# A transformer stack in fp32: the program opens with the MLA input projection, and the memory keys and values come after it

## The chip, the core and the metric

The kernel runs on 1 core of one Trainium2 chip. The metric is the device time of one execution in microseconds (us), as the median of a few runs. Before the change it is 1916.09 us (3 runs, 1915.34 to 1917.74).

Engines are named as in the profile: PE is TensorE's matmuls, PEld its weight loads, DVE VectorE, ACT ScalarE, POOL GpSimd, SP the engine that issues the DMAs.

## What is computed

Two blocks on x (512 tokens, 1024 wide), in fp32. The first block has two layers, each with a mixer, a cross-attention to 256 memory tokens, an output projection and an MLP. The mixer of layer 0 is MLA, that of layer 1 sliding-window attention. The second block (sparse attention, convolutions, FFN) is not touched. What matters here, cut from the reference:

```python
mem_n = rmsnorm(mem, mem_norm_g)
hn = rmsnorm(x, attn_norm_g[0])
proj = hn @ mla_w_in                  # 1024 x 928: c_q 384, c_kv 256, k_r 32, q_cross 256
q  = rmsnorm(c_q, q_norm_g) @ w_uq
kv = rmsnorm(c_kv, kv_norm_g) @ w_ukv
k_r = rope(k_r, positions)
kv_mem = mem_n @ w_mem_kv[i]          # for both layers i, 1024 x 512
cross = softmax(q_cross @ k_mem.T) @ v_mem
```

## The kernel before

Every product of two fp32 matrices is three matmuls: both operands are split into a high part `h` and a low part `l`, and `mm` issues h·h, h·l and l·h into one PSUM bank. Activations stand with features on partitions: 8 tiles of 128 x 512 for x (256 for memory). A projection (`dense`) gives a bank to 128 output columns and runs over 8 contraction tiles, so 24 matmuls make one block.

Weights lie in HBM in the order in which they are used (`_weight_plan`), in chunks of 128 x 512 (256 KB). For each chunk SP loads `raw` (4 buffers), ACT casts `h`, and DVE subtracts `l = raw - h` (8 buffers of each). For the keys in `POOL_KEYS` POOL does the subtraction. `Norm.tile` splits a scaled tile (ACT `h`, DVE `l`) and squares it on ACT, and adds the square to a sum. `finish` gives the sum to PE for column sums (`pst<-ones`), to DVE for a chain of 15 small instructions that make the reciprocal root (`rsqrt`), to DVE for a diagonal matrix and to PE for a broadcast (`pst<-pgf,ones`). ACT copies that to the tile R, and each projection's result is multiplied by R when it leaves its bank.

The order on each engine is set by a list scheduler in the kernel (`Trace.schedule`): among instructions that are ready by its own costs, the one recorded first goes first. `later(n)` shifts a place in the record by n. Each engine then runs its list strictly in that order.

In `build`, `setup` loads the constants, memory and x; `mem_phase` norms memory and makes keys (`memk`) and values (`memv`) of both layers; `first_block` norms x with `Norm.all` (name `n0`), then `mla` runs the five blocks `mla_c0` to `mla_c4` (three at first in parallel, then one by one), the norms `nq` and `nkv`, then `mla_kr`, `mla_x0`, `mla_x1` (the cross queries), then cross-attention and MLA.

In the trace nearly all instructions have one line, that of the recorder; names tell them apart. Pages of SBUF are `pgf` and `pgr`, the PSUM banks `psd` (3), `pss` (2), `pst` (2) and `pso` (1), weight parts `raw`, `h` and `l`.

Of the kernel before, what the change touches and what calls it, by code (L numbers as in the profile page):

```python
# [19 lines left out]
KD = 8  # L20
# [7 lines left out]
X_AT = 200  # L28
POOL_KEYS = ("swa_q", "n_a", "uq", "ukv", "mla_")
MEM_AT = 0  # L30
# [8 lines left out]
def _weight_plan():  # L39
    plan = []  # L40

    def add(key, k, c, fn):
        plan.append((key, k, c, fn))
# [16 lines left out]
    add("mla_kr", KD, 64, kr)  # L60
# [66 lines left out]
def _weight_layout():  # L127
    plan = _weight_plan()
    blocks, chunks, off, cur = {}, [], 0, 0
    keyk = {}  # L130
    for key, k, c, _ in plan:
        keyk[key] = k
        for j in range(k):
            if cur + c > CHUNK:
                chunks.append((off, cur))
                off += P * cur
                cur = 0
            blocks[key, j] = (len(chunks), cur, c)
            cur += c
    chunks.append((off, cur))  # L140
    off += P * cur
    return plan, blocks, chunks, off, keyk


def pack_weights(a):
    plan, blocks, chunks, total, _ = _weight_layout()
    w = np.empty(total, np.float32)
    views = [w[o:o + P * n].reshape(P, n) for o, n in chunks]
    for key, k, c, fn in plan:
        m = fn(a)  # L150
        for j in range(k):
            ch, co, _ = blocks[key, j]
            views[ch][:, co:co + c] = m[j * P:(j + 1) * P]
    return w
# [381 lines left out]
class Norm:  # L536
    def __init__(self, net, src, gains, d, name):
# [6 lines left out]
    def tile(self, m, split=True):  # L544
        net, nc = self.net, self.net.nc
        if split:
            self.h[m], self.l[m] = net.split_scaled(self.src[m], self.gains[m], f"{self.name}s{m}")
# [64 lines left out]
class Net:  # L612
    def __init__(self, ctx, tc, aps):
# [11 lines left out]
        for key, k, _, _ in self.plan:  # L625
            for j in range(k):
                self.first_key.setdefault(self.blocks[key, j][0], key)
# [21 lines left out]
    def load_chunk(self, i):  # L649
        nc = self.nc  # L650
# [24 lines left out]
    def split_scaled(self, src, g, name):  # L675
        nc = self.nc
        n = src.shape[-1]
        h = self.pg(name + "h", FR)[:, :n]
        l = self.pg(name + "l", FR)[:, :n]
# [55 lines left out]
    def dense(self, jobs, xh, xl, il=1, n=S, ks=None):  # L735
        i = 0
        while i < len(jobs):
            grp = jobs[i:i + (il if i == 0 else 1)]
            i += len(grp)
            pss = [self.ps("d") for _ in grp]  # L740
# [24 lines left out]
    def setup(self):  # L765
# [6 lines left out]
        mem = [self.pg(f"mem{j}") for j in range(4)]  # L772
        nc.sync.dma_start(self.vecs, self.a["vec"])
        for j in range(4):
            with nc.later(MEM_AT * j):
                nc.sync.dma_start(mem[j], self.a["memT"][:, 2 * j:2 * j + 2, :].rearrange("p a b -> p (a b)"))
        with nc.later(CST_AT):
            nc.sync.dma_start(self.cst, self.a["cst"])
        self.X = [self.keep(f"x{m}", [P, S]) for m in range(KD)]
        for m in range(KD):  # L780
            with nc.later(X_AT):
                nc.sync.dma_start(self.X[m], self.a["xT"][:, m, :])
# [6 lines left out]
        self.memsrc = [mem[k // 2][:, (k % 2) * 256:(k % 2) * 256 + 256] for k in range(KD)]  # L789
# [40 lines left out]
    def mem_phase(self):  # L830
        nc = self.nc
        nm = Norm(self, self.memsrc, self.gains("mem_norm_g", 0, KD), 1024, "mem")
        nm.all()
        self.memk, self.memv = [], []
        for i in range(2):
# [9 lines left out]
            self.dense([(f"memk{i}_{m}", P, kev(m)) for m in range(2)], nm.h, nm.l, il=2 if i == 0 else 1, n=NMEM)  # L845
# [113 lines left out]
    def mla(self, nx, osh, osl):  # L959
# [9 lines left out]
        self.dense([(f"mla_c{m}", P, cev(m)) for m in range(5)], nx.h, nx.l, il=3)  # L969
        nq = Norm(self, c[:3], self.gains("mla_q_norm_g", 0, 3), 384, "nq")  # L970
        nkv = Norm(self, c[3:], self.gains("mla_kv_norm_g", 0, 2), 256, "nkv")
        ch, cl = [], []
        for nn, cc, g in ((nq, c[:3], nq.gains), (nkv, c[3:], nkv.gains)):
# [706 lines left out]
```

## Time and profile before

| | |
|---|---|
| median of 3 runs | 1916.09 us |
| span of the profiled execution | 1914.9 us |
| PE busy | 1856.5 us (97%), 8749 matmuls |
| DVE busy | 1169.7 us (61%) |
| ACT busy | 835.5 us (44%) |
| POOL busy | 388.9 us (20%) |
| mean granted TensorE clock | 0.991 |

The span runs from the first to the last instruction; the page gives no other time for that execution, so what lies around the span is told by the median alone, which is 1.2 us above it. PE is busy nearly everywhere, so time is to be looked for where PE waits or runs at its lower clock.

### The profile page before, as it was taken

What the parts mean: (1) busy time and instruction counts of PE and PEld (TensorE: products, weight loads), DVE (VectorE), ACT (ScalarE), POOL (GpSimd) and SP (SyncE); (2) the same over time, 40 slices, a digit from 0 to 9 for tenths busy, and PEclk for the clock granted to TensorE, in tenths of its full rate; (3) what the DMA queues carried; (4) which work ended last, traced back from release to release, by engine and by line L of the source; (5) the groups of instructions that cost most, each with busy time, mean ns of one, the idle gap of its engine ahead of it and who ended that gap; (6) DMA issues with size and microseconds to landing.
All of it is one profiled execution on the core that took longest, in us unless ns stands there. A gap on an engine that the chain in (4) does not pass through costs nothing.

```text
span 1914.9 us, 25100 instructions
## 1 busy us (share of the span) xinstructions
PE 1856.5 (97%) x8749; PEld 1527.4 (80%) x8749; DVE 1169.7 (61%) x2268; ACT 835.5 (44%) x1674; POOL 388.9 (20%) x431
## 2 busy tenths in 40 slices
PE   6789999999999998999999999999999999999999
PEld 6567688888888876888888887778888888888887
DVE  8588875444446688654444356777755567774652
ACT  7378644332424677443323243447633333332321
POOL 4454320000001354100000040455300122110100
PEclk9899999999999999999999999899999999999999
DMA  6211133333333210333333322311133233333332
GB/s 214 79 49 50 45 94 104 95 99 95 98 99 95 78 56 17 99 105 95 98 98 95 99 81 58 105 45 45 56 94 99 89 93 105 94 99 99 94 99 76
DMA packets 92150, 166.98 MB, mean 87 GB/s; under 512 B 10612, under 2 KB 12408, under 8 KB 92024
## 3 DMA queue, kind: packets, MB, share of 16 engines
q1 hardware_dynamic: 92024, 165.40, 28.8%
q8 instruction: 68, 1.11, 0.2%
q14 instruction: 58, 0.48, 0.1%
HBM read 161.68 MB, written 2.10 MB: 86 GB/s over the span
## 4 chain that ended last, share of the span: by engine, by line
PE 86%; DVE 7%; ACT 3%; issue 2%; POOL 1%; DMA 1%; SPq 0%; DVEq 0%; POOLq 0%; ACTq 0%
PE psd L415 77%; PE pst L415 3%; DVE pgf L415 3%; PE pso L415 3%; PE pss L415 3%; DVE pgr L415 2%; DVE sm L415 1%; ACT pgf L415 1%; ACT pgr L415 1%; POOL pgf L415 1%; DVE l L415 1%; ACT h L415 1%; DMA raw<-w 0%; DVE x L415 0%; DMA pgf<-memT 0%
## 5 line engine op out<-in xcount | busy, mean ns | idle before, releaser
L415 PE MATMUL psd<-pgr,h 128*128 128x512 f32 (+2 forms) x4622 | 1448.8, 393 | 16.2 <-ACT h L415 11.6
L415 PEld LDWEIGHTS psd<-pgr,h 128*128 128x128 f32 (+1 forms) x4622 | 867.4, 189 | 196.0 <-ACT h L415 11.6
L415 PE MATMUL psd<-pgr,l 128*128 128x512 f32 (+2 forms) x2311 | 905.8, 392 | 0.8 <-DVE l L415 0.8
L415 DVE TENSOR_TENSOR l<-raw,h 128x512 fp32r<-128x512 f32 (+1 forms) x536 | 419.4, 785 | 453.9 <-ACT h L415 451.9
L415 ACT CAST h<-raw 128x512 fp32r<-128x512 f32 (+2 forms) x601 | 368.6, 616 | 700.8 <-PE psd L415 618.5
L415 PEld LDWEIGHTS psd<-pgr,l 128*128 128x128 f32 (+1 forms) x2311 | 436.5, 189 | 91.2 <-issue 3.5
L415 POOL TENSOR_TENSOR pgf<-pgf,pgf 128x512 f32<-128x512 f32 (+1 forms) x106 | 142.3, 1345 | 1078.8 <-ACT pgf L415 770.9
L415 DVE TENSOR_TENSOR pgr<-pgf,pgr 128x512 fp32r<-128x512 f32 (+4 forms) x184 | 130.4, 710 | 14.5 <-ACT pgr L415 9.5
L415 ACT CAST pgr<-pgf 128x512 fp32r<-128x512 f32 (+4 forms) x184 | 108.3, 591 | 58.3 <-POOL pgf L415 31.6
L415 ACT ACTIVATE pgf<-pgf 128x512 f32<-128x512 f32 (+2 forms) x125 | 74.9, 602 | 116.4 <-DVE pgf L415 113.2
L415 DVE TENSOR_TENSOR pgf<-psd,pgf 128x512 f32<-128x512 f32 (+2 forms) x102 | 66.9, 657 | 75.3 <-PE psd L415 73.8
L415 POOL TENSOR_TENSOR l<-raw,h 128x512 fp32r<-128x512 f32 (+1 forms) x65 | 88.8, 1377 | 89.5 <-ACT h L415 68.0
L415 PE MATMUL pso<-pgr,pgr 128*128 128x512 f32 (+3 forms) x368 | 90.6, 341 | 4.2 <-DVE pgf L415 1.8
L415 DVE TENSOR_TENSOR pgr<-pst,pgr 128x512 fp32r<-128x512 f32 (+1 forms) x126 | 74.1, 610 | 15.2 <-ACT pgr L415 14.6
L415 POOL TENSOR_SCALAR pgf<-pgf,sm 128x256 f32<-128x256 f32 (+3 forms) x128 | 70.1, 566 | 65.5 <-DVE sm L415 49.6
L415 PE MATMUL pst<-cstt,pgf 128*128 128x128 f32 x436 | 77.7, 277 | 2.6 <-POOL pgf L415 1.5
L415 ACT CAST pgr<-pst 128x512 fp32r<-128x512 f32 (+1 forms) x126 | 63.3, 529 | 28.2 <-PE pst L415 26.8
L415 PE MATMUL pss<-pgr,pgr 128*128 128x256 f32 (+4 forms) x320 | 69.1, 315 | 6.1 <-DVE sm L415 4.0
L415 PEld LDWEIGHTS pso<-pgr,pgr 128*128 128x128 f32 x368 | 58.4, 189 | 19.6 <-ACT pgr L415 7.3
L415 DVE CUSTOM_DVE_ANT_0 pgf<-pss,cmask 128x256 f32<-128x256 f32 (+3 forms) x144 | 65.7, 469 | 12.9 <-PE pss L415 10.8
L415 ACT ACTIVATE pgf<-pgf,sm 128x256 f32<-128x256 f32 (+3 forms) x128 | 65.9, 516 | 16.0 <-DVE sm L415 15.5
L415 PEld LDWEIGHTS pst<-cstt,pgf 128*128 128x128 f32 x436 | 52.7, 140 | 20.5 <-POOL pgf L415 8.3
(115 smaller groups left out, 1122.8 us busy)
## 6 DMA issues: line engine op xcount, KB each, us to landing
raw<-w SPq DMA_DIRECT2D x588, 256.0 KB, 2.6
x<-xT SPq DMA_DIRECT2D x8, 256.0 KB, 5.6
out<-x SPq DMA_DIRECT2D x8, 256.0 KB, 2.0
pgf<-pgf SPq DMA_DIRECT2D x24, 64.0 KB, 2.0
pgf<-aux SPq DMA_DIRECT2D x5, 256.0 KB, 2.7
pgf<-memT SPq DMA_DIRECT2D x4, 256.0 KB, 4.4
raw<-w SPq DMA_DIRECT2D x7, 140.0 KB, 2.1
raw<-w SPq DMA_DIRECT2D x4, 192.0 KB, 2.5
```

Source lines behind the costliest of these rows:

```text
L415: getattr(getattr(nc, names[o.eng]), o.method)(*[r(x) for x in o.args], **{k: r(v) for k, v in o.kw.items()})
```

## The change

The record is written in another order.

- `mla` comes first. x is no longer normed ahead of the projection: `dense` gets a function `before(k)` that loads x tiles, splits and squares them as the contraction reaches them. The five blocks `mla_c` run together, contraction tile by contraction tile, in three `psd` and two `pss` banks, and the plan has their weights in that order (`weave`).
- Then the cross queries and `mla_kr`; the multiplications by the norms of c and their splits; then `mem_phase` with `memk` and `memv` of both layers. The memory is loaded and split in `mem_prep`, recorded after the c norms.
- `mla_` leaves `POOL_KEYS`, and the norms `n0`, `nq` and `nkv` add on DVE: 15 subtractions and 10 additions move from POOL to DVE. No instruction is added or removed otherwise.
- Every weight load is recorded 80 places earlier (`AHEAD`), through the whole program.

```diff
-X_AT = 200
-POOL_KEYS = ("swa_q", "n_a", "uq", "ukv", "mla_")
-MEM_AT = 0
+AHEAD = 80
+POOL_KEYS = ("swa_q", "n_a", "uq", "ukv")
...
-    for i in range(2):
-        for m in range(2):
-            add(f"memk{i}_{m}", KD, 128, cols("w_mem_kv", i, m * 128, m * 128 + 128))
-        add(f"memv{i}", KD, 256, cols("w_mem_kv", i, 256, 512))
-    for m in range(5):
-        add(f"mla_c{m}", KD, 128, cols("mla_w_in", 0, m * 128, m * 128 + 128))
+    weave([(f"mla_c{m}", cols("mla_w_in", 0, m * 128, m * 128 + 128)) for m in range(5)], KD, 128)
...
+    add("mla_kr", KD, 64, kr)
+    for i in range(2):
+        weave([(f"memk{i}_{m}", cols("w_mem_kv", i, m * 128, m * 128 + 128)) for m in range(2)], KD, 128)
+        add(f"memv{i}", KD, 256, cols("w_mem_kv", i, 256, 512))
...
     def load_chunk(self, i):
+        with self.nc.later(-AHEAD):
+            self.fetch_chunk(i)
...
-            nc.gpsimd.tensor_tensor(self.acc, self.acc, q, op=OP.add)
+            self.adder.tensor_tensor(self.acc, self.acc, q, op=OP.add)
...
-    def dense(self, jobs, xh, xl, il=1, n=S, ks=None):
+    def dense(self, jobs, xh, xl, il=1, n=S, ks=None, banks="ddd", before=None):
...
             for k in order:
+                if before is not None:
+                    before(k)
                 for (key, m, ev), p in zip(grp, pss):
...
+        def before(k):
+            for j in ((0,), (1, 2), (3, 4), (5, 6), (7,), (), (), ())[k]:
+                if j:
+                    nc.sync.dma_start(self.X[j], self.a["xT"][:, j, :])
+                nx.tile(j)
+                if j == KD - 1:
+                    nx.finish()
+            if k == 5:
+                self.load_positions()
+                tables.extend(self.rope_tables(self.posr, self.cst[:, 640:641], self.cst[:, 641:642], "r32"))
-        self.dense([(f"mla_c{m}", P, cev(m)) for m in range(5)], nx.h, nx.l, il=3)
+        self.dense([(f"mla_c{m}", P, cev(m)) for m in range(5)], nx.h, nx.l, il=5, banks="dddss", before=before)
...
+        nm = self.mem_prep()
+        self.dense([("mla_x0", P, xev), ("mla_x1", P, xev)], nx.h, nx.l)
...
+        self.dense([("mla_kr", 64, krev)], nx.h, nx.l)
+        for nn, cc in ((nq, c[:3]), (nkv, c[3:])):
+            for m in range(len(cc)):
+                nc.vector.tensor_tensor(cc[m], cc[m], nn.R, op=OP.mult)
+                h, l = self.split_scaled(cc[m], nn.gains[m], "cn")
...
+        self.mem_phase(nm)
```

The order on the engines changes at three places that matter. The first is SP at the start of the program. Before:

```order
L415 DMA vecs_74<-vec 128x184
L415 DMA pgf_84<-memT 128x512
L415 DMA pgf_88<-memT 128x512
L415 DMA pgf_90<-memT 128x512
L415 DMA pgf_96<-memT 128x512
L415 DMA cstt_104<-cst 128x648
L415 DMA raw_115<-w 128x512
```

Now (`vecs` holds the gains; the x tile is needed with them for the first split):

```order
L414 DMA raw_76<-w 128x512
L414 DMA raw_86<-w 128x512
L414 DMA raw_88<-w 128x512
L414 DMA raw_90<-w 128x512
L414 DMA x_94<-xT 128x512
L414 DMA vecs_100<-vec 128x184
L414 DMA raw_76<-w 128x512
L414 DMA x_109<-xT 128x512
```

The first weight chunk is now the first DMA instead of the seventh, and the gains come sixth.

The second place is DVE where the norm `n0` of x becomes its reciprocal root (`sm` are the small tiles of that chain). Before, the chain stands between keys of the memory (`pgr`, 64x256) and the rope table (`pgf`, 128x512):

```order
L415 TENSOR_SCALAR sm_0_584<-pst_196 128x4
L415 TENSOR_TENSOR pgr_497<-pgf_117,pgr_497 64x256
L415 TENSOR_SCALAR sm_1_591<-sm_0_584 128x4
L415 TENSOR_TENSOR pgr_497<-pgf_117,pgr_497 64x256
L415 TENSOR_SCALAR sm_2_596<-sm_1_591 128x4
L415 TENSOR_SCALAR pgf_234<-pgf_234,cstt_104 128x512
```

Now it stands between splits of the memory (128x256), weight subtractions (`l`) and the rope table:

```order
L414 TENSOR_SCALAR sm_0_309<-pst_290 128x4
L414 TENSOR_SCALAR pgf_295<-pgf_295,cstt_135 128x512
L414 TENSOR_SCALAR sm_1_315<-sm_0_309 128x4
L414 SCALAR_TENSOR_TENSOR pgr_317<-pgf_268,vecs_100,pgr_298 128x256
L414 TENSOR_SCALAR sm_2_324<-sm_1_315 128x4
L414 TENSOR_SCALAR pgf_327<-pgf_295 128x512
L414 TENSOR_TENSOR sm_1_315<-sm_2_324 128x4
L414 TENSOR_TENSOR l_113<-raw_90,h_111 128x512
```

The chain keeps its 15 links and gets other neighbours. On PE its column sums stand behind 60 of the 120 matmuls of the c blocks, and its broadcast behind 103.

The third place is POOL's first work on tiles. Before, seven additions for the memory's norm are followed by seven for x and then by weight subtractions:

```order
L415 TENSOR_TENSOR pgf_100<-pgf_100,pgf_157 128x256
L415 TENSOR_TENSOR pgf_213<-pgf_213,pgf_234 128x512
L415 TENSOR_TENSOR pgf_213<-pgf_213,pgf_309 128x512
L415 TENSOR_TENSOR pgf_213<-pgf_213,pgf_330 128x512
L415 TENSOR_TENSOR pgf_213<-pgf_213,pgf_84 128x512
L415 TENSOR_TENSOR pgf_213<-pgf_213,pgf_88 128x512
L415 TENSOR_TENSOR pgf_213<-pgf_213,pgf_123 128x512
L415 TENSOR_TENSOR pgf_213<-pgf_213,pgf_96 128x512
L415 TENSOR_TENSOR l_169<-raw_115,h_164 128x512
```

Now:

```order
L414 TENSOR_TENSOR pgf_302<-pgf_302,pgf_238 128x256
L414 TENSOR_SCALAR pgf_283<-pgf_302 32x512
L414 TENSOR_SCALAR pgf_295<-pgf_302 32x512
L414 TENSOR_SCALAR pgf_268<-pgf_302 32x512
L414 TENSOR_SCALAR pgf_292<-pgf_302 32x512
L414 TENSOR_TENSOR l_262<-raw_90,h_242 128x384
```

POOL has seven memory additions, then copies of the rope key, and its first subtraction is for the MLA weights (`uq_r0`).

## Rows read from the trace of the kernel before

**Rows 1.** The page's slices, busy tenths: PE.
```profile
PE   6789999999999998999999999999999999999999
```

**Rows 2.** Waits of PE, 0 to 110 us: us in total, times, longest us.
```profile
PE pst L415 <- DVE pgf L415: 16.0, 3, 11.5
PE psd L415 <- ACT h L415: 11.6, 1, 11.6
PE psd L415 <- ACT pgf L415: 1.9, 1, 1.9
```

**Rows 3.** Busy time by stretch: us, each engine's busy us (instructions), PEclk, DMA share, GB/s.
```profile
11.50:18.50 7.00, 6.84 (x30) 6.53 (x31) 6.64 (x13) 5.73 (x11) 3.13 (x4) 1.00 0.56 177
...
51.70:63.20 11.50, 0.00 (x0) 0.00 (x0) 11.08 (x27) 2.00 (x4) 7.38 (x6) 0.69 0.50 137
63.20:66.30 3.10, 3.08 (x5) 1.83 (x6) 0.00 (x0) 0.97 (x2) 0.00 (x0) 0.51 0.00 0
66.30:110.00 43.70, 39.26 (x177) 30.23 (x176) 25.47 (x58) 14.49 (x25) 21.84 (x19) 1.00 0.21 62
110.00:240.00 130.00, 124.35 (x655) 95.41 (x654) 110.22 (x300) 100.77 (x256) 57.40 (x86) 1.00 0.16 47
```

**Rows 4.** Timeline, PE, two stretches: start, us, instruction.
```profile
30.66 0.28 PE L415 MATMUL psd<-pgr,l 128*128 128x256 f32 x1
...
35.34 0.28 PE L415 MATMUL psd<-pgr,l 128*128 128x256 f32 x1
...
66.55 0.40 PE L415 MATMUL psd<-pgr,l 128*128 128x512 f32 x1
...
72.69 0.39 PE L415 MATMUL psd<-pgr,l 128*128 128x512 f32 x1
```

**Rows 5.** Timeline, PE, sums, broadcasts and the first score.
```profile
85.15 0.95 PE L415 MATMUL pst<-ones,pgf 128*128 128x1 f32 x8
...
91.78 1.12 PE L415 MATMUL pst<-pgf,ones 128*128 128x512 f32 x2 [1.10 <-DVE pgf L415]
...
109.97 0.64 PE L415 MATMUL pss<-pgr,pgr 128*128 128x256 f32 x4
```

**Rows 6.** Timeline of the first us; the landing row is of the DMA view.
```profile
0.74 0.39 SPq L415 DMA_DIRECT2D vecs<-vec  x1
...
3.07 0.43 SPq L415 DMA_DIRECT2D cstt<-cst  x1
...
13.00 0.72 ACT L415 ACTIVATE pgr<-x,vecs 128x512 fp32r<-128x512 f32 x1
...
cstt<-cst SPq DMA_DIRECT2D x1, 324.0 KB, 6.2
```

**Rows 7.** Timeline, DVE: work that the change moves or keeps.
```profile
16.67 0.74 DVE L415 SCALAR_TENSOR_TENSOR pgr<-x,vecs,pgr 128x512 fp32r<-128x512 f32 x1
...
35.53 1.28 DVE L415 TENSOR_TENSOR l<-raw,h 128x512 fp32r<-128x512 f32 x2
...
73.21 2.02 DVE L415 TENSOR_TENSOR pgf<-psd,pgf 128x512 f32<-128x512 f32 x3 [10.05 <-PE psd L415]
...
93.71 1.89 DVE L415 TENSOR_TENSOR pgf<-pgf,pgf 128x512 f32<-128x512 f32 x3
```

**Rows 8.** Groups of POOL and DVE, 50.4 to 59.2 us: busy us, mean ns.
```profile
L415 POOL TENSOR_TENSOR l<-raw,h 128x512 fp32r<-128x512 f32 x6 | 8.6, 1466 | 4.0 <-ACT h L415 4.0
...
L415 DVE TENSOR_TENSOR sm<-sm,sm 128x4 f32<-128x4 f32 x2 | 2.4, 1220 | 0.0
```

**Rows 9.** Timeline, DVE: first and last links of the first norm's chain.
```profile
48.66 0.16 DVE L415 TENSOR_SCALAR sm<-pst 128x4 f32<-128x4 f32 x1
...
62.02 0.16 DVE L415 TENSOR_TENSOR sm<-sm,sm 128x4 f32<-128x4 f32 x1
62.29 0.87 DVE L415 TENSOR_SCALAR pgf<-cstt,sm 128x128 f32<-128x128 f32 x4
```

**Rows 10.** Groups of POOL, 0 to 110 us: busy us, mean ns.
```profile
L415 POOL TENSOR_TENSOR pgf<-pgf,pgf 128x256 f32<-128x256 f32 x7 | 5.8, 833 | 6.1 <-ACT pgf L415 5.7
```

More of the change, by code (lines that the diff above doesn't have):

```diff
@@ L130, in _weight_layout @@
     keyk = {}
[L131 to L139, printed above, removed]
+    for key, j, c, _ in plan:
+        keyk[key] = j + 1
+        if cur + c > CHUNK:
+            chunks.append((off, cur))
+            off += P * cur
+            cur = 0
+        blocks[key, j] = (len(chunks), cur, c)
+        cur += c
     chunks.append((off, cur))
@@ L148, in pack_weights @@
     views = [w[o:o + P * n].reshape(P, n) for o, n in chunks]
[L149 to L153, printed above, removed]
+    mats = {}
+    for key, j, c, fn in plan:
+        if key not in mats:
+            mats[key] = fn(a)
+        ch, co, _ = blocks[key, j]
+        views[ch][:, co:co + c] = mats[key][j * P:(j + 1) * P]
     return w
@@ L546, in tile @@
         if split:
-            self.h[m], self.l[m] = net.split_scaled(self.src[m], self.gains[m], f"{self.name}s{m}")
+            self.h[m], self.l[m] = net.split_scaled(self.src[m], self.gains[m], f"{self.name}s{m}",
+                                                    self.into and self.into[m])
         if self.acc is None:
@@ L624, in __init__ @@
         self.first_key = {}
-        for key, k, _, _ in self.plan:
-            for j in range(k):
-                self.first_key.setdefault(self.blocks[key, j][0], key)
+        for key, j, _, _ in self.plan:
+            self.first_key.setdefault(self.blocks[key, j][0], key)
     def nm(self, s):
@@ L771, in setup @@
         nc.scalar.activation(self.sm("warm", 1), self.ones[:, :1], AF.Exp)
-        mem = [self.pg(f"mem{j}") for j in range(4)]
+        self.X = [self.keep(f"x{m}", [P, S]) for m in range(KD)]
+        nc.sync.dma_start(self.X[0], self.a["xT"][:, 0, :])
         nc.sync.dma_start(self.vecs, self.a["vec"])
-        for j in range(4):
-            with nc.later(MEM_AT * j):
-                nc.sync.dma_start(mem[j], self.a["memT"][:, 2 * j:2 * j + 2, :].rearrange("p a b -> p (a b)"))
         with nc.later(CST_AT):
             nc.sync.dma_start(self.cst, self.a["cst"])
[L779 to L782, printed above, removed]
         self.ident = self.cst[:, 0:128]
@@ L788, in setup, with load_positions @@
         self.swamask = self.cst[:, 384:640]
-        self.memsrc = [mem[k // 2][:, (k % 2) * 256:(k % 2) * 256 + 256] for k in range(KD)]
+    def load_positions(self):
+        nc = self.nc
         self.posr = self.pg("posr", I32)
@@ L828, in rope_tables, with mem_prep, mem_phase @@
         return cos, sin
-    def mem_phase(self):
+    def mem_prep(self):
         nc = self.nc
-        nm = Norm(self, self.memsrc, self.gains("mem_norm_g", 0, KD), 1024, "mem")
+        raw = [self.pg(f"mem{j}") for j in range(4)]
+        hp = [self.pg(f"memh{j}", FR) for j in range(4)]
+        lp = [self.pg(f"meml{j}", FR) for j in range(4)]
+        half = lambda t, k: t[k // 2][:, (k % 2) * 256:(k % 2) * 256 + 256]
+        for j in range(4):
+            nc.sync.dma_start(raw[j], self.a["memT"][:, 2 * j:2 * j + 2, :].rearrange("p a b -> p (a b)"))
+        src = [half(raw, k) for k in range(KD)]
+        nm = Norm(self, src, self.gains("mem_norm_g", 0, KD), 1024, "mem",
+                  [(half(hp, k), half(lp, k)) for k in range(KD)])
         nm.all()
+        return nm
+    def mem_phase(self, nm):
+        nc = self.nc
         self.memk, self.memv = [], []
```

54 lines of the change are left out of this document (25 added, 29 removed).

## The prediction

> **What bounds the kernel now.** I read the page's slices first: PE is busy at 9 tenths or more from the fourth slice to the end, nearly without a break, and below that only in the first three, at 6, 7 and 8 [rows 1]. So the opening is where an order can gain. The waits of PE up to 110 us say who is waited for [rows 2]: DVE's diagonal matrices for 16.0 us (one wait of 11.5), the first weight part for 11.6 us, a memory value's eviction for 1.9 us. The stretches [rows 3] add the clock. Up to 18.5 us the 30 recorded matmuls took 6.84 us, which at the later spacing is 3.6; in the 11.5 us wait PE has nothing at all while DVE is busy for 11.08, and the 3.1 us behind it run at a granted clock of 0.51, its lower level. So in the opening DVE is the limit, then PE waits, then DVE idles: from 66.3 to 110 us DVE is busy for only 25.5 of 43.7 us.
>
> As the end of the opening I take the first score of the cross-attention, at 109.97 us [rows 5]. In both orders 401 matmuls stand ahead of it, the same ones, so PE's work up to there is the same: 192 of 512 columns and 192 of 256 for the blocks, the rest column sums and broadcasts. From the spacing of every third matmul, 512 columns take (72.69 - 66.55)/27 = 0.227 us and 256 columns (35.34 - 30.66)/39 = 0.12 us [rows 4]. That is 43.6 + 23.0 us; with the sums (0.95 us for eight) and broadcasts (1.12 us each) [rows 5], some 7.5 us, the work is 74.1 us. So 109.97 - 74.1 = 35.9 us are lost now: 11.6 of start, 3.2 of low clock, 16.0 and 1.9 of waits, 1.2 of low clock behind the long wait, 2.0 of small gaps.
>
> **The change, part by part**, as what PE loses up to the same score.
>
> *Start.* Now the gains and x's first tile come after four weight chunks. The gains are the sixth issue, as the constants were: from 0.74 us on, one each 0.47 us, so at 3.07. The constants landed 6.2 us after that, at 9.3, as the last of 92 + 4 x 256 + 324 = 1440 KB [rows 6]. Up to the gains it is now 5 x 256 + 92 = 1372 KB, so I expect them at 9.0. ACT has cast the weights by then; the split of x takes 0.72 us [rows 6], and with two hand-overs the first matmul comes at 10.0 us, for 11.6. Bounds: 9.0 and 11.6.
>
> *Low clock.* 6.9 us after the first matmul the spacing halved, and I take the same: 16 matmuls of 512 columns at 0.43 us instead of 0.227, so 3.3 us lost. Bounds 2 and 5.
>
> *The first norm.* The c blocks no longer wait for all of x. x comes at under 1 us a tile and PE spends 15 x 0.227 = 3.4 us on each contraction tile, so transfers are covered. So is DVE until the column sums: 8 subtractions at 0.64, 8 splits at 0.74 and 7 additions at 0.63 us [rows 7] are 15.5 us, done near 24, while PE reaches the sums after 60 matmuls: 10.0 + 6.9 + 44 x 0.227 = 26.9. The chain starts at 27.4. PE comes to its broadcast 43 matmuls later, at 37.2. Now the chain took 13.6 us from its first link to the diagonals and 0.9 for them [rows 9], with six POOL subtractions beside it. Under those a link takes 1.22 us instead of 0.16 [rows 8, 9], so each costs DVE about 1.06 us: 6.4 in all, and clean it would be near 8. Its new neighbours are 2 subtractions (1.3 us), 6 half-wide splits (2.4), 7 instructions of the rope table (3.7); with 15 links at 0.2 us, partly beside them, I get 10.2 us with the diagonals. POOL's seven memory additions, 0.83 us each [rows 10], fall in this stretch; at the same share lost (1.06 of 1.47) all would cost 4.2 us, and since ACT spaces them I take 3.0. The diagonals are ready at 27.4 + 13.2 = 40.6, and PE waits 3.4 us. Bounds: 0 (clean and short) and 7.
>
> By the Trainium skill (SBUF — State Buffer, Who interferes with whom), a VectorE instruction with two SBUF inputs and a GpSimd instruction that reads SBUF exclude each other for the whole instruction. By that rule each addition could hold DVE for its full 0.83 us: 5.8 instead of 3.0, a wait of 6.2 us, and 1903.8 us in the sum. The trace shows the mechanism (1.22 for 0.16), not that every addition meets such an instruction, so I keep 3.0.
>
> *Norms of c and memory.* After the last c matmul PE has 12 matmuls of the cross queries (2.7 us) before it needs the sums of c. DVE has five evictions (2.02/3 = 0.67 each), two additions and two subtractions (0.63 and 0.64), 5.9 us, of which I put 1.7 beside the last c blocks. That leaves 1.5 us of waiting, and behind it stand three chains at once; the memory's broadcast is perhaps 0.6 us late. 2.1 us; bounds 0 and 5. Now the same norms cost 1.1 + 3.3 us, the other two waits on diagonals [rows 2].
>
> *Memory last.* Its weights come at 12 matmuls of 256 columns, 1.44 us, a chunk. DVE brings each at 0.64 us, but has the c splits, the query stacks, the rope key and the memory's keys beside them, and near the end four POOL subtractions (1.47 us) lie beside it. By the order DVE's last `memv1` subtraction would be about 2 us late. 2.0 us; bounds 0 and 6.
>
> *15 subtractions and 10 additions moved to DVE* are 15 x 0.64 + 10 x 0.63 = 15.9 us of DVE. They are counted in the waits above; their cover is DVE's idle time from 66.3 us on, now filled. *Memory eviction wait*: gone, since keys run when their scales are long there. *Loads 80 places earlier*: nothing. The eight buffers hold a load back more than its place does, and in the stage after the opening PE idles 5.65 of 130 us [rows 3]. The first softmaxes and `wo` chunks stand in the same succession, within a few rows.
>
> Sum: 10.0 + 3.3 + 3.4 + 2.1 + 2.0 = 20.8 us lost for 35.9, so 15.1 us are won, and the first score comes at 94.9. The profiled span of 1914.9 us becomes 1899.8; the median, 1.2 us above it, becomes **1901.0 us**.
>
> **The rivals.**
> 1. *All waits vanish.* The chain meets no POOL addition, and DVE keeps up: 10.0 + 3.3 us, with 0.5 and 0.5 for the rest, is 14.3 lost, 1894.5 us; with an earlier start 1892. For it: DVE idles for 18 us of the opening now. Against: all 25 moved instructions are DVE's.
> 2. *DVE stays the bound.* If the 15.9 us of moved work came out of PE's time but for what POOL gives back (the 6.4 us of the long chain), 9.5 us would come on top of waits of 1.6 us or so in place of 7.5. That is 24.4 lost, 1904.6; with the bounds of the last three terms (7, 5, 6) 31.3 lost, 1911.5 us. For it: DVE works for 50 of the first 52 us already. Against: its idle 18 us behind.
> 3. *The weights of the attention come late, and it gets slower.* The memory weights now stand right ahead of the attention's, so the first MLA chunks get buffers only as `memv1` gives them up, and POOL subtracts them at 1.47 us beside its 16 normalizations of the cross-attention. DVE, ACT and POOL are busy there for 110, 101 and 57 of 130 us. Some 14 chunks are used there; if each came 1.4 us late, 19.6 us would be lost, more than the 15.1 won, and the time is 1920.6 us. It decides from 1.1 us a chunk on. Against: PE's order mixes scores and projections as before, so that there is other work.
>
> **How the numbers follow.** A measurement here tells 0.2%, 3.8 us, from no change, so faster ends at 1912.3 and slower begins at 1919.9. Forecast 0.62 (1895 to 1907, all faster); rival 1 0.13 (faster); rival 2 0.18 (0.13 faster, 0.05 same); rival 3 0.07 (0.05 slower, 0.02 same). So faster 0.88, same 0.07, slower 0.05. The range runs from 1891 (rival 1, with its early start) to 1911 (rival 2 short of its worst); what is left out are rival 3, some of rival 2 and the far side of rival 1.
>
> **What would show it.** First matmul near 10 us; spacing halved near 17; one wait of PE on a diagonal near 37 us of 2 to 5 us, in place of 11.5 near 52; the first score near 95 us; DVE busy for over 9 tenths from 10 to 90 us, POOL idle for most of the first 80. From the first score to the end the time should be as now, 1805 us within 3. The forecast is wrong if the first score comes before 88 or after 103 us, or if that rest grows or shrinks by more than 4 us.

## The result, and the profile after

The changed kernel took 1888.75 us (4 runs, 1887.60 to 1890.25); the kernel before, in the same comparison, 1915.71. The ratio is 0.9856, with a 95% interval from 0.9842 to 0.9870. That is 27.0 us less, where 15.1 were forecast, and below the stated range.

The page's slices of the changed kernel, PE and DVE, to be held against [rows 1]:

```profile
PE   7999999999999998999999999999999999999998
DVE  8977954444546688544434367777755567774752
```

PE is at 9 tenths from the second slice on, two slices earlier than before. The waits of PE up to the first score, which answer to [rows 2]:

```profile
PE psd L414 <- ACT pgr L414: 8.4, 1, 8.4
PE pst L414 <- DVE pgf L414: 2.6, 1, 2.6
```

Two are left: the start, 8.4 us for 11.6, and one wait on diagonal matrices, 2.6 us for three of 16.0. The timeline of PE tells where they lie; the last row is the first score, at 109.97 us before [rows 5]:

```profile
25.04 0.95 PE L414 MATMUL pst<-ones,pgf 128*128 128x1 f32 x8
...
38.45 1.97 PE L414 MATMUL pst<-pgf,ones 128*128 128x512 f32 x2 [2.55 <-DVE pgf L414]
...
55.90 1.02 PE L414 MATMUL pst<-pgf,ones 128*128 128x512 f32 x2
56.35 1.02 PE L414 MATMUL psd<-pgr,h 128*128 128x512 f32 x2
57.21 0.40 PE L414 MATMUL psd<-pgr,l 128*128 128x512 f32 x1
...
88.92 0.64 PE L414 MATMUL pss<-pgr,pgr 128*128 128x256 f32 x4
```

The first score comes 21.05 us earlier. From there to the end of the span it is 1887.34 - 88.92 = 1798.4 us, for 1914.95 - 109.97 = 1805.0 before: 6.6 us that the forecast did not have. The busy time of the stretches answers to [rows 3] (us, each engine's busy us and instructions, PEclk, DMA share, GB/s):

```profile
8.40:14.80 6.40, 6.38 (x15) 5.02 (x16) 5.79 (x9) 5.26 (x9) 0.75 (x1) 1.00 0.99 332
38.40:42.00 3.60, 3.55 (x7) 2.16 (x8) 2.82 (x6) 1.80 (x4) 0.00 (x0) 0.53 0.00 0
42.00:88.92 46.92, 46.92 (x304) 41.00 (x303) 44.93 (x122) 28.53 (x55) 8.44 (x8) 1.00 0.38 110
0.00:88.92 88.92, 77.95 (x420) 65.41 (x421) 78.21 (x195) 57.43 (x109) 15.77 (x21) 0.98 0.50 155
```

The first row gives a granted clock of 1.00, but the trace has no record of the clock ahead of 14.6 us, and the 15 matmuls of this row stand 0.43 us apart, as the projection's matmuls in the second row do at 0.53; I count them as low clock. The second row is low clock behind the wait on the diagonals. From 42 us to the first score DVE is busy for 44.93 of 46.92 us, and PE for all of it: DVE is full and never late. The last row holds what has to be explained. The same stretch of the kernel before, from its start to its first score, reads:

```profile
0.00:109.97 109.97, 79.39 (x420) 66.23 (x421) 82.03 (x165) 56.24 (x108) 54.37 (x49) 0.95 0.43 134
```

DVE has 30 instructions more in its row now and is busy for 78.21 us instead of 82.03. Work was moved to it, and its time got less.

### The profile page after: what moved, and what is told of

It is laid out like the page before. It is cut to its first block, busy times and chain, and to the rows that moved or that the text cites. A ratio compares the mean times of both kernels' runs of the same rounds, so it can differ in the third digit from the quotient of the medians.

```text
span 1887.3 us, 25092 instructions
## 1 busy us (share of the span) xinstructions
PE 1848.9 (98%) x8749; PEld 1522.6 (81%) x8749; DVE 1163.5 (62%) x2293; ACT 836.9 (44%) x1674; POOL 354.3 (19%) x406
## 4 chain that ended last, share of the span: by engine, by line
PE 89%; DVE 7%; ACT 2%; issue 1%; DMA 1%; POOL 0%; SPq 0%; DVEq 0%; ACTq 0%; POOLq 0%
PE psd L414 79%; PE pst L414 4%; PE pss L414 3%; DVE pgf L414 3%; PE pso L414 3%; DVE pgr L414 2%; DVE l L414 1%; DVE sm L414 1%; ACT pgf L414 1%; ACT pgr L414 0%; DMA raw<-w 0%; DVE x L414 0%; POOL pgf L414 0%; SPq L414 0%; ACT h L414 0%
## 5 line engine op out<-in xcount | busy, mean ns | idle before, releaser
L414 PE MATMUL psd<-pgr,h 128*128 128x512 f32 (+1 forms) x4590 | 1435.2, 392 | 13.1 <-ACT pgr L414 12.0
L414 PEld LDWEIGHTS psd<-pgr,h 128*128 128x128 f32 x4590 | 858.7, 188 | 191.5 <-ACT pgr L414 13.1
L414 PE MATMUL psd<-pgr,l 128*128 128x512 f32 (+1 forms) x2295 | 897.0, 391 | 0.0
L414 DVE TENSOR_TENSOR l<-raw,h 128x512 fp32r<-128x512 f32 (+1 forms) x551 | 430.1, 783 | 457.1 <-ACT h L414 455.0
L414 PEld LDWEIGHTS psd<-pgr,l 128*128 128x128 f32 x2295 | 432.3, 188 | 88.3 <-issue 1.9
L414 POOL TENSOR_TENSOR pgf<-pgf,pgf 128x512 f32<-128x512 f32 (+1 forms) x96 | 128.5, 1342 | 1058.4 <-ACT pgf L414 769.9
L414 DVE TENSOR_TENSOR pgr<-pst,pgr 128x512 fp32r<-128x512 f32 (+1 forms) x126 | 73.8, 610 | 14.3 <-ACT pgr L414 14.1
L414 POOL TENSOR_TENSOR l<-raw,h 128x512 fp32r<-128x512 f32 (+1 forms) x50 | 67.4, 1357 | 75.4 <-ACT h L414 43.7
L414 PEld LDWEIGHTS pso<-pgr,pgr 128*128 128x128 f32 x368 | 58.4, 189 | 19.6 <-ACT pgr L414 7.2
```

What stands on the lines that cost most here:

```text
L414: getattr(getattr(nc, names[o.eng]), o.method)(*[r(x) for x in o.args], **{k: r(v) for k, v in o.kw.items()})
```

## The experiments

The table has every kernel that ran: the median, its ratio to the kernel before (95% interval), and from the profile the time of the first score and the rest of the span. Each ratio is to the kernel before as it ran in the same comparison (medians of 1914.52 to 1915.71 us), and differences to the kernel before are to that median; those to the changed kernel are to 1888.75, whatever the comparison (its second run, after_again, took 1887.56). The first score and the rest are from one execution each; two of the changed kernel have the first score at 88.92 and 87.03 us, so differences of 2 us there tell nothing.

| kernel | us | ratio | first score | rest |
|---|---|---|---|---|
| before | 1915.71 | | 109.97 | 1805.0 |
| changed | 1888.75 | 0.9856 (0.9842 to 0.9870) | 88.92 | 1798.4 |
| order_alone | 1906.65 | 0.9959 (0.9944 to 0.9973) | 103.19 | 1802.2 |
| ahead0 | 1894.60 | 0.9890 (0.9876 to 0.9905) | 88.90 | 1802.1 |
| pool25 | 1901.84 | 0.9930 (0.9913 to 0.9947) | 101.48 | 1799.7 |
| before_dve25 | 1900.22 | 0.9923 (0.9908 to 0.9938) | 95.84 | 1802.6 |
| before_sub15 | 1903.32 | 0.9941 (0.9927 to 0.9956) | 100.80 | 1802.7 |
| before_add10 | 1912.45 | 0.9989 (0.9979 to 0.9999) | 108.49 | 1800.6 |
| before_ahead | 1918.24 | 1.0017 (1.0007 to 1.0027) | 116.86 | 1799.7 |
| pool_dummy | 1893.36 | 0.9887 (0.9873 to 0.9902) | 94.03 | 1796.0 |
| memadd_dve | 1885.77 | 0.9848 (0.9833 to 0.9863) | 85.55 | 1797.1 |
| three_banks | 1897.91 | 0.9908 (0.9892 to 0.9925) | 96.62 | 1800.8 |
| x_first_mem | 1888.57 | 0.9860 (0.9845 to 0.9875) | 87.87 | 1798.9 |
| x_first_mem_keys | 1887.15 | 0.9852 (0.9838 to 0.9867) | 89.12 | 1796.2 |
| ahead_open | 1887.71 | 0.9851 (0.9836 to 0.9866) | 87.50 | 1798.6 |
| after_again | 1887.56 | 0.9851 (0.9835 to 0.9868) | 87.03 | 1798.4 |
| mem_kr_act | 1890.79 | 0.9868 (0.9854 to 0.9883) | 85.03 | 1804.2 |

### The three parts of the change, each undone or alone

The look-ahead undone (ahead0):

```diff
-AHEAD = 80
+AHEAD = 0
```

> The changed kernel with weight loads recorded at their own place again (AHEAD 0). Theory: the look-ahead gives nothing in the opening (first score within 1 us of 88.9), but it is what altered the order in the second block's sparse attention, where the changed kernel is 2.7 us ahead; undone, the time is 1891.5 us, and the stretch from 1136 to 1280 us is as long as before. Rival: weights first at the start is what brings the first matmul to 8.4 us; then the first matmul comes at 11 us or later and the time is 1894. Second rival: what was gained behind the opening is only where the low-clock stretches happen to fall; then 1889 within 2.

Measured: 1894.60 us, 5.9 more. That is the first rival's time, but not for its reason: the first matmul comes at 5.92 us and not at 11 or later, and the first score does not move. The theory's place was wrong too: from the first score to the 1291st recorded matmul, in the first MLP, the changed kernel needs 175.6 us and this one 181.4; behind that this profile has 2 us less.

The 25 instructions back on POOL (pool25):

```diff
-POOL_KEYS = ("swa_q", "n_a", "uq", "ukv")
+POOL_KEYS = ("swa_q", "n_a", "uq", "ukv", "mla_")
...
-nq = Norm(..., adder="vector")     # the same for nkv and n0
+nq = Norm(...)
```

> The changed kernel with the 15 subtractions and 10 additions back on POOL. Theory: the new order covers the first norm only because DVE adds (0.6 us) where POOL took 1.3; back on POOL the column sums come about 6 us later and the chain meets POOL's subtractions, so the wait on the first diagonals grows from 2.6 to 7 to 10 us and one more of 1 to 2 us comes with the norms of c: 1896 to 1899 us. Rival: DVE, at 45 of 47 us from 42 to 89 us, is the bound of the opening; then taking 15.9 us of work from it costs nothing or gains up to 2 us, 1887 to 1889.

Measured: 1901.84 us, 13.1 more than the changed kernel; more than the theory, and the rival is out. The waits of PE up to its first score:

```profile
PE pst L414 <- DVE pgf L414: 11.6, 2, 8.6
PE psd L414 <- ACT pgr L414: 8.4, 1, 8.4
```

The first link of the chain comes at 36.44 us instead of 26.02, and links beside POOL's subtractions take 1.2 us. Two rows of its DVE timeline, one link beside POOL and one not:

```profile
40.07 1.22 DVE L414 TENSOR_SCALAR sm<-sm 128x4 f32<-128x4 f32 x1
...
43.99 0.17 DVE L414 TENSOR_SCALAR sm<-sm 128x4 f32<-128x4 f32 x1
```

The kernel before with the look-ahead alone (before_ahead):

```diff
     def load_chunk(self, i):
+        with self.nc.later(-80):
+            self.fetch_chunk(i)
+
+    def fetch_chunk(self, i):
```

> The kernel before with weight loads recorded 80 places earlier and nothing else. Theory: the start moves by 1 to 2 us and the sparse attention gains 2.7 us, 1911.5 to 1912.5 us; the 11.5 us wait on the first diagonals stays. Rival (low-clock stretches by chance): 1914 to 1916.

Measured: 1918.24 us, slower. The first matmul comes 3.4 us earlier and the first score 6.9 us later. A memory value's eviction is now waited for 7.9 us and not 1.9, and more of the stretch to the first score runs at the lower clock (0.88 granted in the mean, 0.95 in the kernel before):

```profile
PE pst L415 <- DVE pgf L415: 16.8, 3, 12.4
PE psd L415 <- ACT pgr L415: 8.2, 1, 8.2
PE psd L415 <- ACT pgf L415: 7.9, 1, 7.9
```

The kernel before with the 25 instructions on DVE, and nothing else (before_dve25):

```diff
-POOL_KEYS = ("swa_q", "n_a", "uq", "ukv", "mla_")
+POOL_KEYS = ("swa_q", "n_a", "uq", "ukv")
...
-            nc.gpsimd.tensor_tensor(self.acc, self.acc, q, op=OP.add)
+            self.adder.tensor_tensor(self.acc, self.acc, q, op=OP.add)   # vector for n0, nq, nkv
```

> The kernel before with the 25 instructions on DVE and nothing else. Theory: the long chain loses its POOL neighbours (6.4 us) but DVE, busy for 50 of the first 52 us, gets the additions and part of the subtractions there, 8 to 10 us, so the wait of 11.5 us stays within 3 us and the time is 1914 to 1918: the moves alone give nothing. Rival: the contention was the cause of the wait; then it falls to 5 us and the time to 1909.

Measured: 1900.22 us, 14.3 less than the kernel before, in the old order. The theory fell, and the rival was still too small. The three waits on diagonals, 16.0 us [rows 2], are 2.9:

```profile
PE psd L415 <- ACT h L415: 11.5, 1, 11.5
PE pst L415 <- DVE pgf L415: 2.9, 2, 1.5
PE psd L415 <- ACT pgf L415: 2.3, 1, 2.3
```

Why is seen in the groups of DVE (busy us, mean ns of one). First the kernel before, 0 to 110 us:

```profile
L415 DVE SCALAR_TENSOR_TENSOR pgr<-x,vecs,pgr 128x512 fp32r<-128x512 f32 x8 | 9.3, 1164 | 0.1
L415 DVE TENSOR_TENSOR pgr<-pgf,pgr 64x256 fp32r<-64x256 f32 x12 | 8.1, 672 | 0.2
L415 DVE TENSOR_TENSOR sm<-sm,sm 128x4 f32<-128x4 f32 x18 | 5.5, 304 | 0.5
```

Then this kernel, to its first score:

```profile
L415 DVE SCALAR_TENSOR_TENSOR pgr<-x,vecs,pgr 128x512 fp32r<-128x512 f32 x8 | 6.0, 751 | 0.9 <-ACT pgr L415 0.9
L415 DVE TENSOR_TENSOR pgr<-pgf,pgr 64x256 fp32r<-64x256 f32 x12 | 5.0, 418 | 0.2
L415 DVE TENSOR_TENSOR sm<-sm,sm 128x4 f32<-128x4 f32 x18 | 2.8, 160 | 0.4
```

And its busy time in that stretch:

```profile
0.00:95.84 95.84, 77.94 (x423) 65.63 (x423) 78.31 (x192) 56.90 (x110) 18.75 (x24) 1.00 0.50 154
```

The splits of x, the key stacks and the chain's links did the same work in 13.8 us that took 22.9. Over the whole opening DVE took on 15.9 us of work, by the prediction's estimate of 0.64 and 0.63 us each, and went from 82.03 us busy to 78.31: POOL's 54.37 - 18.75 = 35.6 us had cost DVE 82.03 + 15.9 - 78.31 = 19.6 us, an estimate, 0.55 us for each.

The new order alone (order_alone: ahead0 and pool25 together):

> The changed kernel with the 25 instructions back on POOL and weight loads at their own place: the new order of the record alone. Theory: the parts add up as found so far; with the 25 on POOL the changed kernel took 1901.8 us, and the look-ahead was worth 5.8 us there, so 1905 to 1908 us, some 8 us less than before, which is half of what the 25 instructions gave alone in the old order. Rival: in the new order the look-ahead only pays beside a full DVE; then 1900 to 1903.

Measured: 1906.65 us, as the theory said. So from the kernel before (1915.33 in that comparison) the order gives 8.7 us, the 25 instructions 12.1 (to ahead0), the look-ahead 5.9 (to the changed kernel). These shares hold for this order of adding them: alone in the old order the 25 instructions gave 14.3 us and the look-ahead cost 3.7, and with the 25 on POOL the look-ahead gives 4.8 (1906.65 to 1901.84).

### Subtractions or additions

before_sub15 has only the first half of the diff of before_dve25, before_add10 only the second.

> The kernel before with the 15 weight subtractions alone on DVE. Theory: the chain of the first norm starts as late as before (48 to 49 us) but loses its six POOL neighbours, 13.6 us become 9 to 10, and the subtractions take the time of additional DVE work after it: 6 to 8 us gained, 1907 to 1909. Rival: the additions alone made the gain; then 1913 or more.

> The kernel before with the ten additions of the three norms alone on DVE. Theory: the chain starts 5 us earlier, at 43 to 44 us, but still meets POOL's subtractions; 5 to 6 us gained, 1909 to 1910, so that the two parts add up to the 14 us of both. Rival: the subtractions alone made the gain; then 1913 or more.

Measured: 1903.32 and 1912.45 us, 11.9 and 2.7 less than the kernel before; together 14.6, for 14.3 of both at once. The subtractions gave more than I expected and the additions less, and the reason given for the additions was wrong: it is without the subtractions that the chain starts early, at 44.28 us for 48.66 [rows 9], because DVE's work right ahead of it, key stacks and rope table, no longer lies beside POOL's subtractions. One instruction of the rope table, in the kernel before and in before_sub15:

```profile
42.15 1.67 DVE L415 SCALAR_TENSOR_TENSOR pgf<-pgf,pgf 128x512 f32<-128x512 f32 x1
```

```profile
41.91 0.68 DVE L415 SCALAR_TENSOR_TENSOR pgf<-pgf,pgf 128x512 f32<-128x512 f32 x1
```

The column sums that the chain reads are issued at 42.9 us in both. With the additions alone on DVE the sums come 0.9 us earlier, all splits of x take 0.75 us, and the chain still starts at 49.74.

### POOL's work that nobody waits for

The changed kernel with ten more additions on POOL, on a spare page (pool_dummy):

```diff
+        scr = self.pg("scr")
+        for _ in range(10):
+            nc.gpsimd.tensor_tensor(scr, nx.R, nx.R, op=OP.add)
         nm = self.mem_prep()
```

> The changed kernel with ten additions of 128x512 more on POOL, on a spare page, reading the broadcast norm of x and read by nobody; they lie from about 41 us on, where POOL has nothing to do. The order of all other engines is the same. Theory: what POOL's work cost in the kernel before was not only that it was late but that it slows DVE beside it; ten of 1.45 us, 14.5 us, at the 0.4 to 0.5 us lost on DVE per us of POOL that the kernel before and its version with the 25 on DVE show, make DVE 6 to 7 us later where it is busy for 45 of 47 us, and the first score comes 4 to 7 us later: 1893 to 1896 us. Rival: only POOL's lateness counts, nobody waits for these, and the time stays within 1 us of 1888.8.

Measured: 1893.36 us, 4.6 more, as the theory said; lateness is out as the only cause. PE, DVE and ACT run the changed kernel's lists, instruction for instruction. Groups of DVE from 41 to 57 us in the changed kernel, where POOL has nothing to do:

```profile
L414 DVE TENSOR_TENSOR l<-raw,h 128x512 fp32r<-128x512 f32 x5 | 3.4, 686 | 0.0
L414 DVE TENSOR_TENSOR pgf<-psd,pgf 128x512 f32<-128x512 f32 x4 | 2.8, 690 | 0.5 <-PE psd L414 0.5
L414 DVE TENSOR_TENSOR pgf<-pgf,pgf 128x512 f32<-128x512 f32 x3 | 2.0, 687 | 0.0
```

And in this one:

```profile
L414 DVE TENSOR_TENSOR l<-raw,h 128x512 fp32r<-128x512 f32 x5 | 5.0, 1003 | 0.0
L414 DVE TENSOR_TENSOR pgf<-pgf,pgf 128x512 f32<-128x512 f32 x3 | 3.7, 1270 | 0.0
L414 DVE TENSOR_TENSOR pgf<-psd,pgf 128x512 f32<-128x512 f32 x3 | 1.9, 676 | 0.0
```

The group of the ten additions there, and the busy time up to the first score:

```profile
L414 POOL TENSOR_TENSOR pgf<-pgf 128x512 f32<-128x512 f32 x10 | 12.3, 1227 | 7.3 <-ACT pgf L414 6.6
```

```profile
0.00:94.03 94.03, 78.43 (x420) 66.38 (x421) 83.86 (x195) 57.52 (x109) 28.16 (x31) 0.96 0.47 146
```

An addition of two tiles in SBUF goes from 687 to 1270 ns, about as long as one of POOL's (1227); an eviction, which reads one operand from PSUM, does not change (690 and 676). DVE is busy for 83.86 us up to the first score instead of 78.21 with the same 195 instructions, and that score comes 5.1 us later. By the Trainium skill (SBUF — State Buffer, Who interferes with whom), a VectorE instruction with two SBUF inputs and a GpSimd instruction that reads SBUF shut each other out, and a VectorE instruction with at most one SBUF input, outside the 2-port perf modes, is free of that. Both halves agree with these rows. The link at 40.07 us in pool25 has one SBUF input and paid (1.22 us for 0.17); no run here shows in which mode it ran.

The memory's seven additions on DVE as well (memadd_dve), so that POOL is silent beside the first chain:

```diff
-                  [(half(hp, k), half(lp, k)) for k in range(KD)])
+                  [(half(hp, k), half(lp, k)) for k in range(KD)], adder="vector")
```

> The changed kernel with the seven additions of the memory's norm on DVE too, so that POOL does nothing beside the first norm's chain. Theory: the seven slow links (0.70 us beside POOL, 0.15 without) become fast, 3.9 us, for 2.8 us of additions of which half lie in the chain; the wait of 2.6 us falls to 0 to 1.5, its low clock goes: 1886 to 1887.5 us. Rival: DVE is full there and takes the additions out of PE's time: 1890 to 1892.

Measured: 1885.77 us (1884.45 to 1886.40), a little beyond the theory. The chain, first two links and diagonals, in the changed kernel:

```profile
26.02 0.16 DVE L414 TENSOR_SCALAR sm<-pst 128x4 f32<-128x4 f32 x1 [2.44 <-PE pst L414]
...
26.75 0.71 DVE L414 TENSOR_SCALAR sm<-sm 128x4 int32<-128x4 int32 x1
...
37.44 0.86 DVE L414 TENSOR_SCALAR pgf<-cstt,sm 128x128 f32<-128x128 f32 x4
```

and in this one:

```profile
24.81 0.16 DVE L414 TENSOR_SCALAR sm<-pst 128x4 f32<-128x4 f32 x1 [1.65 <-PE pst L414]
...
25.29 0.16 DVE L414 TENSOR_SCALAR sm<-sm 128x4 int32<-128x4 int32 x1
...
32.58 0.86 DVE L414 TENSOR_SCALAR pgf<-cstt,sm 128x128 f32<-128x128 f32 x4
```

12.3 us become 8.6. Up to 32.5 us seven instructions of the chain's stretch, among them five links of 0.70 us, hold DVE up beside POOL's additions, 3.5 us in sum over what the same instructions take here; the rest is two additions more (0.7 us) and two half-wide splits less (0.8 us). The wait of 2.6 us is gone, and a wait of 1.7 us on a memory subtraction is new. This is the fastest kernel measured, 2 to 3 us ahead of the changed one; the intervals of their ratios overlap.

### What five banks do

three_banks runs `mla_c0` to `mla_c2` together, and `mla_c3` and `mla_c4` behind them.

```diff
-    weave([... for m in range(5)], KD, 128)
+    weave([... for m in range(3)], KD, 128)
+    for m in (3, 4):
+        add(f"mla_c{m}", KD, 128, ...)
...
-    self.dense([... for m in range(5)], nx.h, nx.l, il=5, banks="dddss", before=before)
+    self.dense([... for m in range(5)], nx.h, nx.l, il=3, before=before)
```

> The changed kernel with three of the five c blocks run together, in the three psd banks, and the other two one by one behind them, their weights in that order. Theory: five banks give PE 43 matmuls between the column sums of x and the broadcast, 10 us; with three there are 24, 5.4 us, for a chain of 12 us, so the wait of 2.6 us grows to 7 to 9 us with low clock behind it: first score at 93 to 96 us, 1893 to 1897 us. Rival: the chain isn't what five banks cover, since PE finds other blocks; then within 1.5 us of 1888.8.

Measured: 1897.91 us, first score at 96.62, just beyond the upper ends of the theory. PE now waits 2.7 us for the diagonals and, right ahead of that, 5.1 us for the memory's sums, which the scheduler put there:

```profile
31.95 1.01 PE L416 MATMUL pst<-ones,pgf 128*128 128x1 f32 x4 [5.12 <-POOL pgf L416]
35.67 2.04 PE L416 MATMUL pst<-pgf,ones 128*128 128x512 f32 x2 [2.71 <-DVE pgf L416]
```

The diagonals are ready at 35.5 us, so without the sums PE would have stood there just as long, from 26.8 us on. Five banks put matmuls into that time. With three, the changed kernel is hardly ahead of before_dve25, which has the old order (1897.91 and 1900.22 us, overlapping intervals): of the 11.5 us between that kernel and the changed one, 9.2 go with the five banks.

### Three attempts to gain more

x_first_mem is memadd_dve with the gains and x's first tile ahead of the weights on SP:

```diff
+        with nc.later(-200):
+            nc.sync.dma_start(self.vecs, self.a["vec"])
+            nc.sync.dma_start(self.X[0], self.a["xT"][:, 0, :])
```

> The changed kernel with the memory's additions on DVE and the gains and x's first tile ahead of the first four weight chunks on SP. Theory: the first matmul comes near 5.9 us, as in the run without look-ahead, instead of 7.8, but weights behind it still come in time, and DVE's chain starts 1 to 2 us earlier: 1883.5 to 1885 us. Rival: x's last tile and DVE's splits set the chain, as where the look-ahead was undone (first matmul 2.5 us earlier, first score not earlier); then the same as with the memory's additions alone, 1885.8 within 0.7.

Measured: 1888.57 us, slower than memadd_dve by 2.8: neither. The first matmul comes at 6.5 us instead of 7.8, and what is won is lost near 67 us, where PE waits 3.3 us for a memory subtraction and runs at its lower clock behind it (0.64 granted from 66.6 to 76.0 us). The matmul that waits, here and in memadd_dve:

```profile
69.93 0.58 PE L414 MATMUL psd<-l,pgr 128*128 128x256 f32 x1 [3.33 <-DVE l L414]
```

```profile
70.12 0.39 PE L414 MATMUL psd<-l,pgr 128*128 128x256 f32 x1 [1.65 <-DVE l L414]
```

PE gets there 1.9 us earlier, but DVE's subtraction comes only 0.2 us earlier: DVE is busy for 22.94 of the 24 us from 42 to 66 us and has no time to spare, so an earlier start gives nothing.

x_first_mem_keys moves the subtractions of `uq` and `ukv` to DVE too:

```diff
-POOL_KEYS = ("swa_q", "n_a", "uq", "ukv")
+POOL_KEYS = ("swa_q", "n_a")
```

> The same, with the 14 weight subtractions of the MLA's up projections moved from POOL to DVE as well. Theory: POOL's work slows DVE by 0.35 to 0.45 us for each us, so each of 1.45 us costs DVE some 0.6 us anyway and moving it is free: from the first score to the first output projection the time stays within 1 us, and the last two memory values no longer meet POOL, 0 to 2 us gained. Rival: DVE, with the softmax, is the limit there; then 4 to 8 us lost.

Measured: 1887.15 us. From the first score to the 1291st matmul it is 175.2 us for 175.7 in x_first_mem: the move costs nothing beside the softmax, as the theory said. The gain at the memory values did not come (first score 89.12 us for 87.87).

mem_kr_act is memadd_dve with the rope key's copies on ACT:

```diff
-                    nc.gpsimd.tensor_scalar(K[h][64:96], kr[64:96], 1.0, 1.0, op0=OP.mult, op1=OP.mult)
+                    nc.scalar.copy(K[h][64:96], kr[64:96])
```

> The changed kernel with the memory's additions on DVE and the twelve copies of the rope key on ACT instead of POOL. Theory: four of the copies lie at 60 to 68 us beside DVE's densest stretch and slow it (1.09 us for 0.68); without them the wait of 1.8 us on a subtraction near 68 us goes and the first score comes 1 to 2.5 us earlier: 1883.5 to 1885 us. Rival: ACT, which casts the weights that DVE waits for, is late by what it takes over; then 1886 or more.

Measured: 1890.79 us, the rival's time, but not its reason. The first score gains 0.5 us, which tells nothing, and the stretch from there to the 1291st matmul takes 182.9 us for 176.2. ACT isn't late at the longest wait there; it idles for 2.5 us itself, for DVE. Four subtractions of POOL, three copies of DVE and the matmul that waits for DVE's next small tile:

```profile
109.67 5.53 POOL L414 TENSOR_TENSOR l<-raw,h 128x512 fp32r<-128x512 f32 x4
```

```profile
112.15 3.33 DVE L414 COPY pgf<-pgf 32x512 f32<-32x512 f32 x3
```

```profile
116.46 0.92 PE L414 MATMUL pss<-pgf,pgf 96*128 96x384 f32 x1 [1.86 <-DVE sm L414]
```

In memadd_dve POOL is idle until the last of these copies has started, and they take 0.42 us each. Behind the wait the granted clock is 0.51 from 116.5 to 123.5 us. What makes up the rest of the 6.7 us I have not found.

### What the look-ahead does, and what repeats

ahead_open gives the look-ahead to the opening's loads only:

```diff
-        with self.nc.later(-AHEAD):
+        k = self.first_key[i]
+        with self.nc.later(-AHEAD if k.startswith(("mla", "mem")) else 0):
```

> The changed kernel with the 80 places of look-ahead for the weights of the MLA input and the memory alone; all later loads at their own place. Up to the second block's sparse attention every engine's order is the changed kernel's, in the sparse attention it is that of the kernel before. Theory: the 5.8 us of the look-ahead come from the opening's loads, by the order that they leave for the first attention; the order in the sparse attention is worth nothing, and where low clock falls there is chance: 1887.5 to 1890. Rival: the changed order in the sparse attention is what gains behind the first attention; then 1891 to 1893.

Measured: 1887.71 us, as the theory said: the later loads' look-ahead is worth nothing that can be told. after_again is the changed kernel a second time.

> The changed kernel once more, for a second profile. Theory: the wait of 2.6 us, the first score at 88.9 us and the stretch from there to the first output projection repeat within 0.5 us; the short low-clock stretches behind it (one near 735 us in the kernel before, none in the first profile of the changed kernel) fall otherwise, so that of the 6.6 us gained behind the opening 3.5 repeat and the other 3 do not. Rival: all 6.6 us repeat within 1 us.

Measured: 1887.56 us. Its wait on the diagonals is again 2.6 us, but behind it the granted clock is full:

```profile
37.00:41.00 4.00, 3.24 (x12) 2.37 (x13) 3.16 (x10) 3.13 (x6) 0.00 (x0) 1.00 0.00 2
```

The first score comes at 87.03 us, 1.9 earlier, so that part of the theory fell. The broadcast behind the wait is already 0.7 us earlier (37.76 for 38.45), since fewer matmuls at the start stand 0.43 us apart, 9 for 15, though the first comes 0.4 us later. From the first score on all 6.6 us repeat (1798.4 us): the rival. They fall into two parts. 179.06 - 175.58 = 3.5 us lie between the first score and the 1291st matmul; the seven profiles with the look-ahead in the opening, five banks and the 25 instructions on DVE (mem_kr_act apart) have 175.2 to 176.2 there. Where one or two of the three are missing it is more: 181.4 in ahead0, 178.5 in pool25, 178.6 in three_banks, 179.1 in order_alone. Six of the seven have one and the same order of matmuls in that stretch; x_first_mem_keys and those with longer times have others. The other 3 us lie behind it. There all kernels, whatever was changed, take between 1620.7 and 1625.9 us, PE has one of only two orders, neither always ahead, and the profile of the kernel before is the 1625.9; I count those as scatter.

## Why the prediction was wrong

**The sum.** The forecast fell short by 11.9 us (27.0 for 15.1), about half of it ahead of the first score and half behind, where it had nothing. It had 20.8 us lost up to the first score, at 94.9 us; that came at 88.92. The 6.0 us between are, step by step: start 1.6, low clock 0.3, the wait on the diagonals 0.8, the norms of c and memory 2.1, memory last 2.0, PE's own work some 1.0 (a pair of broadcasts takes 0.86 us of PE, 55.90 to 57.21 less two matmuls of 0.227, and not 1.12), less 1.8 for low clock behind the wait, which I had left out.

- **Start: mis-sized, 8.4 for 10.0 us.** I had let the gains land at 9.0 us, 5.9 after their issue, from the 6.2 us of the constants [rows 6] and the bytes ahead of both. They landed 4.3 us after it, by the DMA view of 0 to 40 us:

```profile
vecs<-vec SPq DMA_DIRECT2D x1, 92.0 KB, 4.3
```

- **Low clock: right, by luck.** 15 matmuls in the first 6.4 us, 3.0 us lost for 3.3; in the second profile of the same kernel it was 9 matmuls and some 1.8 us.
- **The first norm: right in size, by errors that partly cancel.** PE waited 2.6 us for 3.4, and chain and diagonals took 12.3 us for 13.2. POOL's part of them was 3.5 us and not 3.0, the rest 8.8 and not 10.2. By the rule of the Trainium skill (SBUF — State Buffer, Who interferes with whom) I had estimated 5.8 us for POOL's part; the measurement lies between 3.0 and that.
- **The failing step: "15 subtractions and 10 additions moved to DVE are 15.9 us of DVE. They are counted in the waits above."** That counts only one side. I had read in the chain that six POOL subtractions cost DVE 6.4 us, gave it back there, and nowhere else. The rows of the kernel before had it everywhere: a split of x at 0.74 us in [rows 7] and 1164 ns in the mean of eight. Counted over the opening, the POOL work that before_dve25 moves had cost DVE some 19.6 us, more than the 15.9 that it brings. So the waits of 2.1 and 2.0 us, which stood for a loaded DVE, were 0, and before_dve25 alone won 14.3 us, nearly what I had forecast for the whole change.
- **"Loads 80 places earlier: nothing": failed, 5.9 us.** Not by loads that come earlier in the later program, which ahead_open leaves at their place, but by the opening's: with their look-ahead the scheduler leaves another order for the first attention. It pays only together with the five banks and the 25 on DVE: alone in the old order it cost 3.7 us. What in that order saves the time stays open. Of the 5.8 us between ahead0 and the changed kernel there, 1.5 are waits of PE (4.8 and 3.3) and some 1.7 are low clock (0.96 granted from 89 to 130 us in ahead0, 1.00 in the changed kernel); the other 2.6 I can't place.
- **Signs.** One wait on a diagonal of 2 to 5 us, DVE over 9 tenths, POOL idle for most of the first 80 us, a halved spacing: all as written. The first matmul came at 8.4 us for 10, and the wait ended at 38.45 us instead of "near 37". The first score, 88.92 for 95, was still inside its bounds of 88 and 103. The rest of the program, 1805 us within 3 and wrong beyond 4, was the sign that failed: it shrank by 6.6.
- **Two readings were wrong and changed nothing in the sum.** 420 matmuls stand ahead of the first score in the traces of both kernels, not 401, as the counts of the last row and of the kernel before above show. And DVE's "50 of the first 52 us" are 50.4 of the 51.7 us from 11.5 to 63.2 us; in the first 52 it is busy for 45.8.

**Rivals.** The first was the closest: all waits vanish but one, and 88.92 - 74.1 = 14.8 us were lost for its 14.3. In the second DVE is the bound at 24.4 us lost or more; DVE is full, at 44.93 of 46.92 us, but not late. x_first_mem shows how near it is. The third, late attention weights, did not come: that stretch got shorter.

## What to carry to other kernels

Where POOL and DVE both work on tiles in SBUF, moving work from POOL to DVE is to be priced with what POOL's instructions cost DVE now: compare the mean of each DVE form in the crowded stretch with the same form elsewhere in the trace. Here each us on POOL cost 0.46 to 0.55 us of DVE, and DVE did the moved work in less than half of POOL's time (0.64 us for 1.47), so the move was free even where DVE was 95% busy. And where PE is fed by an engine that is nearly full, an earlier start of PE was worth nothing in the two runs that had one (ahead0 and x_first_mem): what was won ahead of that engine was lost at it.

## What was not expected of the hardware

- Ten POOL additions that nobody reads cost 5.1 us at the first score; per us of POOL DVE lost (83.86 - 78.21)/(28.16 - 15.77) = 0.46 us.
- A link of 128x4, 0.17 us, takes 1.22 us beside POOL: the small instruction pays 1.05 us for a POOL subtraction of 1.47 [rows 8], and evictions from PSUM pay nothing (690 and 676 ns).
- The same wait of 2.6 us was followed by a granted clock at its lower level in one profile of the changed kernel (0.53 from 38.4 to 42.0 us) and not in the other (1.00 from 37.0 to 41.0). With the shorter low clock at the start that moved the first score by 1.9 us.
